# Four weight tiles instead of three in the slab-wise first products of a two-layer decoder trunk, and a later row broadcast

## The chip, the core and the metric

One core of a Trainium2 chip runs the whole program. Its engines have queues of their own: PE (TensorE: matmuls), DVE (VectorE), ACT (ScalarE), POOL (GpSimd) and SP, which issues most loads. The metric is the device time of one execution in microseconds. Before the change it is 2145.63 us, the median of three runs (2145.09 to 2147.61).

## What is computed

A decoder trunk of two layers over 512 positions of width 1024, in float32. Each layer has four sub-layers, and each of these adds a normalised output to the residual x:

```
for i in range(DEPTH):                                   # 2
    h = rmsnorm(x, g_ffn1_pre[i])
    x = x + 0.5 * rmsnorm(swiglu(h, w1_gate[i], w1_up[i], w1_down[i]), g_ffn1_post[i])   # 1024 -> 2816 -> 1024
    h = rmsnorm(x, g_mix_pre[i])
    ... = split(h @ w_in[i])                             # three head groups: two attentions, a short convolution
    x = x + rmsnorm(concatenate([y_sb, y_mla, y_cv]) @ w_out[i], g_mix_post[i])
    h = rmsnorm(x, g_ffn2_pre[i])
    x = x + 0.5 * rmsnorm(swiglu(h, w2_gate[i], w2_up[i], w2_down[i]), g_ffn2_post[i])
    h = rmsnorm(x, g_ple_pre[i])
    e = sigmoid(h @ w_ple_gate[i]) * (p[i] @ w_ple_proj[i])
    x = x + rmsnorm(e, g_ple_post[i])
```

with `rmsnorm(x, g) = x * rsqrt(mean(x * x) + 1e-6) * g`.

## The kernel before

Everything is held transposed: 128 channels on the partitions, the 512 positions along the free side, so x is eight tiles (slabs, k = 0 to 7) of 128 x 512. A float32 product is made of three matmuls of rounded halves: high weights with high activations, high weights with low activations, low weights with high activations (`product`, L286 to L288). High halves of weights (wh) are casts on ACT (L270), low halves (wl) a subtraction on DVE or POOL (L271); one such instruction covers 128 x 512, four slabs of a tile. A weight tile is 1024 x 128: eight slabs, two loads of 256 KB, two wh and two wl. There are 4 buffers for raw loads and 8 each for wh and wl, so four whole tiles at a time.

At the seven boundaries between sub-layers the work is split in two halves of the positions, A and B (256 columns each). The old stage ends in `finish`: its output is scaled by the reciprocal root of its mean square. For each half, the roots rt are worked out by nine small DVE instructions (L369), spread over the partitions by transposes on PE (L402, "the row"), copied by ACT (L403, rbs), and multiplied into the output (L579, DVE and POOL by turns). Then x is updated (L583 or L586), and the new stage's input is split: the high half xh on ACT (L467), the low half xl on DVE (L470), and ACT squares x for the next norm. `Entry` does this: `half` for one half, slab by slab.

The new stage doesn't wait for its own norm. `Entry.products` multiplies the first `FIRST` weight tiles with half A slab by slab, as soon as a slab is there: for each slab k the products of xh with wh and wl of every tile (L488, L489), and one slab later (`LAG`) those of xl with wh (L493). This order on PE is written out by hand. After slab `ROW_AT` comes the row of half B of the old stage (`row_b`), which DVE needs to start on half B; the rest of half A follows. Half B of the same tiles comes then, by `product`. `more` adds `MORE` further tiles, whole: 24 matmuls of 512 columns each; their casts and subtractions are held back by `later` until the last high and low half of half A are issued. Then the sums of squares of both halves go through PE as one-column matmuls (st, L389), DVE makes the new stage's own roots, and their row (the "full row") is broadcast when the stage calls `state.row()`.

The FFN computes eight tiles in plain products before its main loop: tiles 0 to 2 in `products`, 3 in `more`, 4 and 5 before the full row and 6 and 7 behind it. The mixer has four tiles before the value products (vt, L1111 to L1113): three in `products`, one in `more`. The embedding (`ple`) has three tiles and eight projections in `more`. The first FFN of layer 0 has no stage before it and uses a start of its own with three tiles. All other instructions are ordered by a scheduler that works from priorities and its own estimates; only the PE and DVE parts marked `manual_schedule` are fixed.

The letters in `ON_FFN1`, `ON_FFN2`, `ON_MIX` and `ON_PLE` say for each tile where its two wl are made: v on DVE, g on POOL.

Of the kernel before, what the change touches and what calls it, by code (L numbers as in the profile page):

```python
# [33 lines left out]
AT_END = (8, 16)  # L34

FIRST = 3
ROW_AT = 5
MORE = 1
LAG = 1
PROJ = 8  # L40
LAST_POOL = (2, 6)
DIRECT = 2

ON_FFN1 = 'vv gg vg'
ON_FFN2 = 'vv vv vv'
ON_MIX = 'vg vg vg'
ON_PLE = 'vv vg vg'
ON_IN = 'vv'
ON_VT = 'v'
# [52 lines left out]
PLAIN_BANKS = "zsfzzsdf"  # L102
# [56 lines left out]
def hybrid_trunk(ctx: ExitStack, tc: tile.TileContext, a: dict, out: bass.AP):  # L159
# [9 lines left out]
    def slot(dt=F32, name="s", tag="s"):  # L169
        return sp.tile([P, S], dt, tag=tag, name=name, bufs=SLOTS[tag])  # L170
# [6 lines left out]
    def bank(name="ps", tag=None):  # L177
        if tag is None:
            tag = dense[0][turn[0] % len(dense[0])]
            turn[0] += 1  # L180
        return ps.tile([P, S], F32, tag=tag, name=name, bufs=BANKS[tag])
# [13 lines left out]
    def split(src, tag="s"):  # L195

        h, lo = slot(F32R, "h", tag), slot(F32R, "l", tag)
        A.copy(out=h, in_=src)
        V.tensor_tensor(out=lo, in0=src, in1=f(h), op=ALU.subtract)  # L199
        return h, lo  # L200
# [26 lines left out]
    def round_constants():  # L227
        tri = slot(name="tri")
        nc.scalar.dma_start(out=tri, in_=a["const"][:, C_MS:C_MS + 4 * P])
        A.copy(out=conr[:, 0:P], in_=ident)  # L230
        A.copy(out=conr[:, P:5 * P], in_=tri)
# [12 lines left out]
    def load_w(src, slabs, cols, on="vv", tag=None):  # L244


        per = S // cols
        return [w for k0 in range(0, slabs, per)
                for w in halves(load_raw(src[:, k0:min(k0 + per, slabs)], cols), on[k0 // per % len(on)], tag)]
# [29 lines left out]
    def product(o, w, xs, first=True, cols=slice(0, S), tick=lambda: None, last=True):  # L279

        oc = o[:, cols]
        n = len(xs)
        for k in range(n):
            (wh, wl), (xh, xl) = w[k], xs[k]
            kw = dict(skip_group_check=True)
            T.matmul(oc, wh, xh[:, cols], start=first and k == 0, stop=False, **kw)  # L286
            T.matmul(oc, wh, xl[:, cols], start=False, stop=False, **kw)  # L287
            product.last = T.matmul(oc, wl, xh[:, cols], start=False, stop=last and k == n - 1, **kw)  # L288
            tick()

    def start():

        def load(t, c):
            m, j = divmod(t, 2)
            raw[t, c] = load_raw(a["w1_gu"][0, m, j][:, 4 * c:4 * c + 4], P)

        def part(k):
            g = gain(0, "ffn1_pre", k)
            h, lo = xs[k]
            A.activation(out=h, in_=x[k], func=AF.Copy, scale=g)  # L300
            V.scalar_tensor_tensor(out=lo, in0=x[k], scalar=g, in1=f(h), op0=ALU.mult, op1=ALU.subtract)

        xs = [(slot(F32R, "xh"), slot(F32R, "xl")) for _ in range(NK)]
        raw, w = {}, {}
        for k, tc_ in enumerate(((0, 0), (1, 0), (0, 1), (1, 1))):
            load(*tc_)
            load_x(k + 1)
        load_x(*range(5, NK))
        load_constants()
        for k, t in enumerate(((0, 0), (1, 0), (0, 1), (1, 1))):  # L310
            part(k)
            w[t] = halves(raw[t])
        for k, c in ((4, 0), (6, 1)):
            load(2, c)
            part(k)
            w[2, c] = halves(raw[2, c])
            part(k + 1)
        first = [(w[t, 0] + w[t, 1], bank("ps", PLAIN_BANKS[t])) for t in range(3)]
        for k in range(NK):
            for w_, o in first:  # L320
                product(o, w_[k:k + 1], xs[k:k + 1], k == 0, last=k == NK - 1)
        sq = Squares()
        for k in range(NK):
            sq.add(x[k])
        sq.fold()
        eps = eps_col()
        r = Rstd(D, keep=eps)
        r.add(*sq.parts(), last=True)
        r.col()
        behind = rsqrt_cols.last.ins  # L330

        def row():
            rb = slot(name="rb")
            r.row(rb, "v")
            return rb

        return SimpleNamespace(xs=xs, row=row, first=first, eps=eps, behind=behind)
# [112 lines left out]
    class Entry:  # L450
# [27 lines left out]
        def products(self, tiles, more=lambda: None):  # L478
# [3 lines left out]
            with tc.manual_schedule(engines={T.engine}):  # L482

                for k in range(NK + LAG):
# [5 lines left out]
                    if k >= LAG:  # L490
                        j = k - LAG
                        for w, o in tiles:
                            T.matmul(o[:, ca], w[j][0], self.xs[j][1][:, ca], start=False, stop=j == NK - 1, **kw)  # L493
                    if k == ROW_AT:
                        self.row_b()
# [236 lines left out]
    def ffn(l, idx, state, nxt, xtag="s", early=None):  # L732
# [4 lines left out]
        order = [(m, j) for m in range(PLAIN) for j in range(2)]  # L737
        src = a[f"w{idx + 1}_gu"]

        def weights(m, j, on="vv"):  # L740
            return load_w(src[l, m, j], NK, P, on)
# [17 lines left out]
            banks[m, j] = b  # L759

        def more():
            for i in range(FIRST, FIRST + MORE):
                with state.later():
                    w = weights(*order[i])
                banks[order[i]] = bank("ps", PLAIN_BANKS[i])
                product(banks[order[i]], w, xs)
# [5 lines left out]
            u.load("t1")  # L772
            u.load("t3")
        if l == 0 and idx == 0:
            first, done = state.first, FIRST
            round_constants()
        else:
            first = [(weights(*t, on), bank("ps", b))
                     for t, on, b in zip(order[:FIRST], (ON_FFN1, ON_FFN2)[idx].split(), PLAIN_BANKS)]
            state.products(first, more)  # L780
            done = FIRST + MORE
        for t, (_, b) in zip(order, first):
            banks[t] = b
        forms = input_forms(l, f"ffn{idx + 1}_pre", xs, xtag)
# [47 lines left out]
        for m in range(NK - LAST_DOWN):  # L832
            if early is not None and m == TRIG_AT:
                early()
            if m < TOGETHER:
                o = together[m]
            else:
                o = bank()
# [211 lines left out]
    def mixer(l, state, nxt):  # L1050
# [9 lines left out]
        def scaled(o, r, name="c"):  # L1060
            c = slot(name=name)
            V.tensor_tensor(out=c, in0=o, in1=r, op=ALU.mult)
            return c

        def latent(ms, name):
# [9 lines left out]
            if name[4] in FOLD:  # L1075
# [2 lines left out]

        q, kk = [], []
        first = [(load_w(a["win_f"][l, m], NK, P, on), bank("in", t))  # L1080
                 for m, t, on in zip((5, 6, 7, 8)[:FIRST], "zzzf", ON_MIX.split())]
        rest = []

        def more():
            for m, t in ((5, "z"), (6, "z"), (7, "z"), (8, "f"))[FIRST:]:
                with state.later():
                    w = load_w(a["win_f"][l, m], NK, P)
                rest.append(bank("in", t))
                product(rest[-1], w, xs)

        state.products(first, more)
        rt, rb = state.rt, state.row()
        for i in range(4):
            o = first[i][1] if i < FIRST else rest[i - FIRST]
            if i < 2:
                c = slot(name="c")
                V.scalar_tensor_tensor(out=c, in0=o, scalar=0.125, in1=rb, op0=ALU.mult, op1=ALU.mult)
                q.append(split(c, "m"))
            else:
                kk.append(split(scaled(o, rb), "m"))  # L1100
# [17 lines left out]
        for b in range(TB):  # L1118
            o = vt[b]
# [152 lines left out]
        for m in range(NK - LAST_OUT):  # L1272
            o = bank("wo")
# [69 lines left out]
    state = start()  # L1343
    for l in range(DEPTH):
        state = ffn(l, 0, state, (l, "mix_pre"), xtag="m" if l else "s", early=None if l else trig)
        state = mixer(l, state, (l, "ffn2_pre"))
        state = ffn(l, 1, state, (l, "ple_pre"))
        state = ple(l, state, (l + 1, "ffn1_pre") if l + 1 < DEPTH else None)
# [58 lines left out]
```

## Time and profile before

| | |
|---|---|
| median of 3 runs | 2145.63 us |
| the profiled execution | 2147.86 us |
| its span, first to last instruction | 2146.1 us |
| mean granted PE clock | 0.984 |
| PE busy | 2059.6 us, 96% |
| DVE busy | 1553.6 us, 72% |
| ACT busy | 1116.6 us, 52% |
| POOL busy | 506.6 us, 24% |

The profile is of one execution, whose time is 2.2 us over the median. Times in the trace count from the first instruction. A row of the timeline has its start, its duration, engine, line and operation, what is written and read, the shape, and in brackets the engine's idle time before it and what ended that. L numbers are lines of the kernel before; in the changed kernel every line after the constants is two further on.

### The profile page before, as it was taken

The numbers are of one execution on the slowest core, as the hardware profiler recorded it, in microseconds if no ns is written. First come the engines' busy times: TensorE is split into PE (matmuls) and PEld (weight loads), VectorE is DVE, ScalarE is ACT, GpSimd is POOL, SyncE is SP. The second block draws the span as 40 slices with busy tenths as digits, with TensorE's granted clock in tenths as the row PEclk, the third lists the DMA queues.
The fourth block names the chain that finished last, engine by engine and source line by source line (L and its number), as shares of the span: only waits on it lengthen the run. The fifth ranks groups of instructions, "written<-read, shape, count | busy, mean of one in ns | idle before, by whom it ended". The sixth has DMA issues, their size and how long they took to land.

```text
span 2146.1 us, 35942 instructions
## 1 busy us (share of the span) xinstructions
PE 2059.6 (96%) x13264; PEld 1874.2 (87%) x13264; DVE 1553.6 (72%) x2851; ACT 1116.6 (52%) x2296; POOL 506.6 (24%) x498
## 2 busy tenths in 40 slices
PE   8999999999989999999989999999999899999996
PEld 6999988887888999888879998888878889998886
DVE  7888754778878788636798786357788798885376
ACT  6556533555656555524565555235455565564243
POOL 3111012126432111003431110031263421100043
PEclk9999999999999999999999999999999999999998
DMA  7777332211133876332427763322111348753321
GB/s 218 172 180 177 89 104 72 91 60 52 55 79 108 196 173 148 100 99 79 122 84 196 178 163 93 98 68 93 53 59 46 88 126 192 180 137 96 98 73 65
DMA packets 139425, 244.73 MB, mean 114 GB/s; under 512 B 15600, under 2 KB 26096, under 8 KB 139248
## 3 DMA queue, kind: packets, MB, share of 16 engines
q1 hardware_dynamic: 117792, 204.00, 30.9%
q0 software_dynamic: 20736, 37.76, 11.2%
q8 instruction: 104, 1.70, 0.3%
q10 hardware_dynamic: 720, 0.67, 0.1%
q14 instruction: 73, 0.60, 0.1%
HBM read 240.27 MB, written 2.10 MB: 113 GB/s over the span
## 4 chain that ended last, share of the span: by engine, by line
PE 82%; DVE 12%; ACT 2%; issue 1%; DMA 1%; POOL 0%; SPq 0%; DVEq 0%; ACTq 0%; POOLq 0%
PE ps L286 9%; PE ps L287 9%; PE ps L288 9%; PE ux L698 6%; PE ux L697 6%; PE ux L696 6%; PE uy L698 3%; PE uy L697 3%; PE uy L696 3%; PE in L286 2%; PE in L287 2%; PE in L288 2%; DVE xl L470 2%; DVE wl L271 2%; PE uz L698 2%; PE uz L697 2%
## 5 line engine op out<-in xcount | busy, mean ns | idle before, releaser
L271 DVE TENSOR_TENSOR wl<-raw,wh 128x512 fp32r<-128x512 f32 (+2 forms) x893 | 605.8, 692 | 393.4 <-ACT wh L270 340.8
L270 ACT CAST wh<-raw 128x512 fp32r<-128x512 f32 (+1 forms) x934 | 548.7, 605 | 577.9 <-PE ps L287 275.1
L444 POOL TENSOR_TENSOR sq<-sq 128x256 f32<-128x256 f32 (+1 forms) x165 | 172.6, 1046 | 730.5 <-ACT sq L434 726.3
L287 PE MATMUL ps<-l,wh 128*128 128x512 f32 (+1 forms) x824 | 302.2, 367 | 0.0
L288 PE MATMUL ps<-h,wl 128*128 128x512 f32 (+1 forms) x824 | 301.8, 367 | 0.4 <-DVE wl L271 0.4
L286 PE MATMUL ps<-h,wh 128*128 128x512 f32 (+1 forms) x824 | 300.2, 368 | 0.0
L680 POOL DMA_DIRECT2D raw<-in_w_gu x144 | 125.9, 915 | 678.0 <-DMA raw<-in_w_gu 181.8
L698 PE MATMUL ux<-fh,wl 128*128 128x256 f32 x864 | 244.5, 283 | 0.0
L697 PE MATMUL ux<-fl,wh 128*128 128x256 f32 x864 | 244.5, 283 | 0.0
L696 PE MATMUL ux<-fh,wh 128*128 128x256 f32 x864 | 244.4, 283 | 0.0
L288 PEld LDWEIGHTS ps<-h,wl 128*128 128x128 f32 x824 | 155.4, 189 | 25.9 <-DVE wl L271 1.3
L287 PEld LDWEIGHTS ps<-l,wh 128*128 128x128 f32 x824 | 155.5, 189 | 24.8 <-DVE l L199 0.2
L286 PEld LDWEIGHTS ps<-h,wh 128*128 128x128 f32 x824 | 155.4, 189 | 24.6
L696 PEld LDWEIGHTS ux<-fh,wh 128*128 128x128 f32 x864 | 165.8, 192 | 0.5
L697 PEld LDWEIGHTS ux<-fl,wh 128*128 128x128 f32 x864 | 165.8, 192 | 0.5
L698 PEld LDWEIGHTS ux<-fh,wl 128*128 128x128 f32 x864 | 165.8, 192 | 0.0
L286 PE MATMUL ps<-xh,wh 128*128 128x512 f32 (+1 forms) x416 | 133.3, 356 | 15.5 <-ACT wh L270 9.8
L287 PE MATMUL ps<-xl,wh 128*128 128x512 f32 (+1 forms) x416 | 142.0, 352 | 1.2 <-DVE xl L470 1.2
L288 PE MATMUL ps<-xh,wl 128*128 128x512 f32 (+1 forms) x416 | 142.2, 350 | 0.0
L286 PEld LDWEIGHTS ps<-xh,wh 128*128 128x128 f32 x416 | 77.4, 196 | 28.7 <-ACT wh L270 11.2
L686 DVE TENSOR_TENSOR raw<-raw 128x512 f32<-128x512 f32 x144 | 98.6, 684 | 0.1
L287 PEld LDWEIGHTS ps<-xl,wh 128*128 128x128 f32 x416 | 80.6, 194 | 10.4 <-DVE xl L470 2.0
(347 smaller groups left out, 5237.1 us busy)
## 6 DMA issues: line engine op xcount, KB each, us to landing
raw<-in_w_gu SPq DMA_DIRECT2D x424, 256.0 KB, 4.0
raw<-in_w_down SPq DMA_DIRECT2D x160, 256.0 KB, 2.7
raw<-in_w_gu POOLq DMA_DIRECT2D x144, 256.0 KB, 5.1
raw<-in_win_f SPq DMA_DIRECT2D x60, 256.0 KB, 2.7
raw<-in_ple_gate SPq DMA_DIRECT2D x32, 256.0 KB, 2.7
raw<-in_wo_a SPq DMA_DIRECT2D x18, 256.0 KB, 2.8
raw<-in_w_down SPq DMA_DIRECT2D x32, 128.0 KB, 2.2
raw<-in_wo_b SPq DMA_DIRECT2D x12, 256.0 KB, 2.7
```

What stands on the lines that cost most here:

```text
L270: A.copy(out=h, in_=raw)
L271: (G if on == "g" else V).tensor_tensor(out=lo, in0=raw, in1=f(h), op=ALU.subtract)
L286: T.matmul(oc, wh, xh[:, cols], start=first and k == 0, stop=False, **kw)
L287: T.matmul(oc, wh, xl[:, cols], start=False, stop=False, **kw)
L288: product.last = T.matmul(oc, wl, xh[:, cols], start=False, stop=last and k == n - 1, **kw)
L444: G.tensor_tensor(out=self.acc[:, c], in0=self.acc[:, c], in1=self.last[:, c], op=ALU.add)
L470: iv = V.scalar_tensor_tensor(out=lo, in0=x[k][:, c], scalar=g, in1=f(h), op0=ALU.mult, op1=ALU.subtract)
L680: G.dma_start(out=self.raw[n], in_=self.part(m), accum_op=ALU.add)
L686: V.tensor_tensor(out=r, in0=r, in1=self.raw[p], op=ALU.add)
L696: T.matmul(o, wh, xh, start=first and k == 0, stop=False, **kw)
L697: T.matmul(o, wh, xl, start=False, stop=False, **kw)
L698: T.matmul(o, wl, xh, start=False, stop=k == 3, **kw)
```

## The change

`FIRST` stays 3 for the embeddings. FFN and mixer get constants of their own with 4, `MORE` becomes 0, so the fourth tile goes through the two halves like the others, and its casts and subtractions are no longer held back. `ROW_AT` goes from 5 to 7 at all seven boundaries. The fourth entry 'vv' puts both wl of the fourth tile on DVE, where `more` had them too.

```diff
@@ -34,16 +34,18 @@
 AT_END = (8, 16)
 
 FIRST = 3
-ROW_AT = 5
-MORE = 1
+FIRST_FFN = 4
+FIRST_MIX = 4
+ROW_AT = 7
+MORE = 0
 LAG = 1
 PROJ = 8
 LAST_POOL = (2, 6)
 DIRECT = 2
 
-ON_FFN1 = 'vv gg vg'
-ON_FFN2 = 'vv vv vv'
-ON_MIX = 'vg vg vg'
+ON_FFN1 = 'vv gg vg vv'
+ON_FFN2 = 'vv vv vv vv'
+ON_MIX = 'vg vg vg vv'
 ON_PLE = 'vv vg vg'
 ON_IN = 'vv'
 ON_VT = 'v'
@@ -759,7 +761,7 @@
             banks[m, j] = b
 
         def more():
-            for i in range(FIRST, FIRST + MORE):
+            for i in range(FIRST_FFN, FIRST_FFN + MORE):
                 with state.later():
                     w = weights(*order[i])
                 banks[order[i]] = bank("ps", PLAIN_BANKS[i])
@@ -772,13 +774,13 @@
             u.load("t1")
             u.load("t3")
         if l == 0 and idx == 0:
-            first, done = state.first, FIRST
+            first, done = state.first, len(state.first)
             round_constants()
         else:
             first = [(weights(*t, on), bank("ps", b))
-                     for t, on, b in zip(order[:FIRST], (ON_FFN1, ON_FFN2)[idx].split(), PLAIN_BANKS)]
+                     for t, on, b in zip(order[:FIRST_FFN], (ON_FFN1, ON_FFN2)[idx].split(), PLAIN_BANKS)]
             state.products(first, more)
-            done = FIRST + MORE
+            done = FIRST_FFN + MORE
         for t, (_, b) in zip(order, first):
             banks[t] = b
         forms = input_forms(l, f"ffn{idx + 1}_pre", xs, xtag)
@@ -1078,11 +1080,11 @@
 
         q, kk = [], []
         first = [(load_w(a["win_f"][l, m], NK, P, on), bank("in", t))
-                 for m, t, on in zip((5, 6, 7, 8)[:FIRST], "zzzf", ON_MIX.split())]
+                 for m, t, on in zip((5, 6, 7, 8)[:FIRST_MIX], "zzzf", ON_MIX.split())]
         rest = []
 
         def more():
-            for m, t in ((5, "z"), (6, "z"), (7, "z"), (8, "f"))[FIRST:]:
+            for m, t in ((5, "z"), (6, "z"), (7, "z"), (8, "f"))[FIRST_MIX:]:
                 with state.later():
                     w = load_w(a["win_f"][l, m], NK, P)
                 rest.append(bank("in", t))
@@ -1091,7 +1093,7 @@
         state.products(first, more)
         rt, rb = state.rt, state.row()
         for i in range(4):
-            o = first[i][1] if i < FIRST else rest[i - FIRST]
+            o = first[i][1] if i < FIRST_MIX else rest[i - FIRST_MIX]
             if i < 2:
                 c = slot(name="c")
                 V.scalar_tensor_tensor(out=c, in0=o, scalar=0.125, in1=rb, op0=ALU.mult, op1=ALU.mult)
```

The order of DVE at the boundary into mixer 0, before: y is the last output of the old FFN, x_75 to x_78 are slabs 2 to 5 of x.

```order
L470 SCALAR_TENSOR_TENSOR xl<-x_74,gains,xh 128x256
L855 TENSOR_SCALAR y<-ps,half 128x256
L586 TENSOR_TENSOR x_76<-y,x_76 128x256
L470 SCALAR_TENSOR_TENSOR xl<-x_75,gains,xh 128x256
L579 TENSOR_TENSOR y<-y,rbs 128x256
L586 TENSOR_TENSOR x_77<-y,x_77 128x256
L470 SCALAR_TENSOR_TENSOR xl<-x_76,gains,xh 128x256
L586 TENSOR_TENSOR x_78<-y,x_78 128x256
L369 SCALAR_TENSOR_TENSOR r_v<-st,eps 128x2
```

And in the changed kernel at the same place:

```order
L472 SCALAR_TENSOR_TENSOR xl<-x_74,gains,xh 128x256
L857 TENSOR_SCALAR y<-ps,half 128x256
L588 TENSOR_TENSOR x_76<-y,x_76 128x256
L273 TENSOR_TENSOR wl<-raw,wh 128x512 x2
L472 SCALAR_TENSOR_TENSOR xl<-x_75,gains,xh 128x256
L581 TENSOR_TENSOR y<-y,rbs 128x256
L371 SCALAR_TENSOR_TENSOR r_v<-st,eps 128x2
L588 TENSOR_TENSOR x_77<-y,x_77 128x256
L472 SCALAR_TENSOR_TENSOR xl<-x_76,gains,xh 128x256
```

Two wl, those of the fourth tile, now stand between the updates of slab 3 and the low half of slab 2; in the order before they stand behind half A:

```order
L369 TENSOR_TENSOR r_q<-r_v,r_z 128x2
L470 SCALAR_TENSOR_TENSOR xl<-x_80,gains,xh 128x256
L369 TENSOR_TENSOR r_q<-r_q,r_z 128x2
L369 SCALAR_TENSOR_TENSOR r_w<-r_q 128x2
L271 TENSOR_TENSOR wl<-raw,wh 128x512
L369 SCALAR_TENSOR_TENSOR rt<-r_w,r_z 128x2
L271 TENSOR_TENSOR wl<-raw,wh 128x512
L579 TENSOR_TENSOR y<-y,rbs 128x256
L586 TENSOR_TENSOR x_73<-y,x_73 128x256
```

These rows became:

```order
L371 TENSOR_TENSOR r_q<-r_v,r_z 128x2
L472 SCALAR_TENSOR_TENSOR xl<-x_79,gains,xh 128x256
L371 TENSOR_TENSOR r_q<-r_q,r_z 128x2
L371 SCALAR_TENSOR_TENSOR r_w<-r_q 128x2
L472 SCALAR_TENSOR_TENSOR xl<-x_80,gains,xh 128x256
L371 SCALAR_TENSOR_TENSOR rt<-r_w,r_z 128x2
L581 TENSOR_TENSOR y<-y,rbs 128x256
L588 TENSOR_TENSOR x_73<-y,x_73 128x256
L588 TENSOR_TENSOR x_74<-y,x_74 128x256
```

The two wl are gone from there, and the row's L581 follows rt at once.

PE at the same boundary (the output is the mixer's bank in). Before, a slab has three pairs of xh products, with no other matmul between them; the last two pairs of slab 1, the xl products and the start of slab 2:

```order
L488 MATMUL in<-xh,wh 128x256
L489 MATMUL in<-xh,wl 128x256
L488 MATMUL in<-xh,wh 128x256
L489 MATMUL in<-xh,wl 128x256
L493 MATMUL in<-xl,wh 128x256 x3
L488 MATMUL in<-xh,wh 128x256
```

In the changed kernel, the third and fourth pair of slab 0 and the first of slab 1 (st are one-column sums of squares for half B of the old stage):

```order
L490 MATMUL in<-xh,wh 128x256
L491 MATMUL in<-xh,wl 128x256
L490 MATMUL in<-xh,wh 128x256
L391 MATMUL st<-con,sq 128x1 x2
L491 MATMUL in<-xh,wl 128x256
L490 MATMUL in<-xh,wh 128x256
L491 MATMUL in<-xh,wl 128x256
```

The fourth tile's pair of products stands in slab 0, with two of the sums between its two matmuls. At the row of half B, before:

```order
L489 MATMUL in<-xh,wl 128x256
L493 MATMUL in<-xl,wh 128x256 x3
L402 MATMUL rb<-ident,rt 128x128 x2
L488 MATMUL in<-xh,wh 128x256
L489 MATMUL in<-xh,wl 128x256
```

and in the changed kernel:

```order
L491 MATMUL in<-xh,wl 128x256
L495 MATMUL in<-xl,wh 128x256 x4
L404 MATMUL rb<-ident,rt 128x128 x2
L495 MATMUL in<-xl,wh 128x256 x4
L288 MATMUL in<-xh,wh 128x256 x4
```

The row now has only the last slab's four xl products behind it before half B begins.

DVE at the boundary into the second FFN of layer 0 (part is the mixer's output), before:

```order
L579 TENSOR_TENSOR part<-part,rbs 128x256
L1287 TENSOR_TENSOR part<-wo,part 128x256
L583 SCALAR_TENSOR_TENSOR x_75<-part,gains,x_75 128x256
L470 SCALAR_TENSOR_TENSOR xl<-x_74,gains,xh 128x256
L583 SCALAR_TENSOR_TENSOR x_76<-part,gains,x_76 128x256
L470 SCALAR_TENSOR_TENSOR xl<-x_75,gains,xh 128x256
L579 TENSOR_TENSOR part<-part,rbs 128x256
L369 TENSOR_SCALAR r_v<-st 128x2
```

and in the changed kernel:

```order
L581 TENSOR_TENSOR part<-part,rbs 128x256
L1289 TENSOR_TENSOR part<-wo,part 128x256
L273 TENSOR_TENSOR wl<-raw,wh 128x512
L585 SCALAR_TENSOR_TENSOR x_75<-part,gains,x_75 128x256
L273 TENSOR_TENSOR wl<-raw,wh 128x512
L472 SCALAR_TENSOR_TENSOR xl<-x_74,gains,xh 128x256
L585 SCALAR_TENSOR_TENSOR x_76<-part,gains,x_76 128x256
L472 SCALAR_TENSOR_TENSOR xl<-x_75,gains,xh 128x256
L581 TENSOR_TENSOR part<-part,rbs 128x256
```

Here too the two wl of the fourth tile move into half A, one ahead of the update of slab 2 and one behind it.

## The prediction

> **What bounds the kernel now.** I read the page first, then the waits, then windows and the timeline around the seven stage boundaries. From the page and the waits (engine line waited for: us in total, times, longest us):
>
> ```profile
> span 2146.1 us, 35942 instructions
> PE 82%; DVE 12%; ACT 2%; issue 1%; DMA 1%; POOL 0%; SPq 0%; DVEq 0%; ACTq 0%; POOLq 0%
> PE rb L402 <- DVE rt L369: 27.2, 10, 4.4
> ```
>
> PE carries the chain, and DVE takes it over for 12%. The third line names one such place: PE waits for the reciprocal roots rt before it can broadcast them (L402). Seven of its ten cases are row b of the half-entries (start, us, engine and line, in brackets the idle time before and what ended it):
>
> ```profile
> 378.08 0.43 PE L402 MATMUL rb<-ident,rt 128*128 128x128 f32 x2 [3.91 <-DVE rt L369]
> 645.62 0.69 PE L402 MATMUL rb<-ident,rt 128*128 128x128 f32 x2 [3.56 <-DVE rt L369]
> 1010.87 0.43 PE L402 MATMUL rb<-ident,rt 128*128 128x128 f32 x2 [1.93 <-DVE rt L369]
> 1083.49 0.69 PE L402 MATMUL rb<-ident,rt 128*128 128x128 f32 x2 [4.44 <-DVE rt L369]
> 1444.58 0.69 PE L402 MATMUL rb<-ident,rt 128*128 128x128 f32 x2 [2.93 <-DVE rt L369]
> 1713.69 0.69 PE L402 MATMUL rb<-ident,rt 128*128 128x128 f32 x2 [3.56 <-DVE rt L369]
> 2076.18 0.43 PE L402 MATMUL rb<-ident,rt 128*128 128x128 f32 x2 [1.93 <-DVE rt L369]
> ```
>
> In this order: mixer 0, second FFN 0, embedding 0, first FFN 1, mixer 1, second FFN 1, embedding 1; 22.3 us of PE idle. Whether that is time of the kernel depends on who is bound on both sides. Windows (stretch: us, then busy time of PE, PEld, DVE, ACT, POOL, PE clock, DMA share, GB/s), mixer 0 and second FFN 0, each up to row b and behind it:
>
> ```profile
> 363.80:378.08 14.28, 8.27 (x65) 7.66 (x65) 14.14 (x31) 7.75 (x19) 8.49 (x10) 1.00 0.05 13
> 378.08:396.70 18.62, 18.62 (x122) 17.58 (x123) 16.38 (x28) 9.52 (x25) 9.30 (x11) 0.91 0.22 60
> 631.00:645.62 14.62, 9.93 (x76) 9.04 (x76) 14.59 (x33) 10.28 (x25) 10.42 (x12) 0.97 0.12 35
> 645.62:677.06 31.44, 31.44 (x176) 28.32 (x176) 30.65 (x57) 20.62 (x46) 11.68 (x13) 0.90 0.38 105
> ```
>
> Up to row b DVE is the bound (14.14 of 14.28, 14.59 of 14.62). Behind it the mixer is PE's (18.62 of 18.62), while in the FFN both are full (DVE 30.65 of 31.44). So a filled row wait is no gain as such: it gives PE work that it then need not do later, which helps only where PE is the later of the two.
>
> **The change part by part. PE's work** stays nearly equal:
>
> ```profile
> 365.55 0.28 PE L488 MATMUL in<-xh,wh 128*128 128x256 f32 x1
> 365.67 0.28 PE L489 MATMUL in<-xh,wl 128*128 128x256 f32 x1
> 379.01 0.42 PE L488 MATMUL in<-xh,wh 128*128 128x256 f32 x1
> 379.22 0.41 PE L489 MATMUL in<-xh,wl 128*128 128x256 f32 x1
> 395.10 0.39 PE L286 MATMUL in<-xh,wh 128*128 128x512 f32 x1
> 395.33 0.39 PE L287 MATMUL in<-xl,wh 128*128 128x512 f32 x1
> ```
>
> Matmuls follow each other every 0.12 us with 256 columns and every 0.23 with 512. The fourth tile's 24 x 0.23 = 5.5 us become 48 x 0.12 = 5.8: +0.3 per boundary. Rows three and four are the same matmul 0.21 apart: after a mostly idle stretch PE runs at half clock for a window.
>
> **The fourth tile's weights come late.** Its first low halves (wl, a DVE subtraction for four slabs) stand in DVE's new order where the front part shows them, in the middle of half A's updates. DVE in mixer 0 and second FFN 0:
>
> ```profile
> 368.19 0.47 DVE L855 TENSOR_SCALAR y<-ps,half 128x256 f32<-128x256 f32 x1
> 368.59 0.41 DVE L586 TENSOR_TENSOR x<-y,x 128x256 f32<-128x256 f32 x1
> 368.92 0.96 DVE L470 SCALAR_TENSOR_TENSOR xl<-x,gains,xh 128x256 fp32r<-128x256 f32 x1
> 377.26 0.69 DVE L271 TENSOR_TENSOR wl<-raw,wh 128x512 fp32r<-128x512 f32 x1
> 635.35 0.41 DVE L1287 TENSOR_TENSOR part<-wo,part 128x256 f32<-128x256 f32 x1
> 635.69 0.64 DVE L583 SCALAR_TENSOR_TENSOR x<-part,gains,x 128x256 f32<-128x256 f32 x1
> ```
>
> Mixer 0: the two wl go in where L470 started, 368.92; the first is done 0.65 later, at 369.55. PE's order is written by hand: slab 0 now has an eighth matmul that needs this wl, at the place where 365.67 stands. PE waits there some 3.9 us; the idle time moves from row b to slab 0. From 369.55 on, one matmul of slab 0, 7 x 8 of slabs 1 to 7 and 7 x 4 low products come before row b: 85 x 0.12 = 10.2, so row b stands at 379.75 at the earliest, 1.7 later than now; rt (two wl of 0.65 ahead of it, one that stood before it gone) moves by 0.65 to about 378.6 and is no longer what PE waits for. If the stall sets the clock to half up to 371.8, as after the row waits now, it is 1.1 more. DVE's half B starts 1.7 to 2.8 later. Second FFN 0: wl at 635.69 + 0.65 = 636.35, plus 10.2, plus 1.45 for the twelve one-column sums that stand there: row b at 648.0, or 649.4 with half clock, against 645.62. DVE's start of half B:
>
> ```profile
> 378.95 0.42 DVE L579 TENSOR_TENSOR y<-y,rbs 128x256 f32<-128x256 f32 x1 [0.33 <-ACT rbs L403]
> 645.49 1.28 DVE L271 TENSOR_TENSOR wl<-raw,wh 128x512 fp32r<-128x512 f32 x2
> 646.75 0.42 DVE L579 TENSOR_TENSOR part<-part,rbs 128x256 f32<-128x256 f32 x1
> ```
>
> In the FFN the row takes about 0.9 us to reach DVE, and now two wl fill those; they have moved forward, so DVE really waits there. Its start goes from 646.75 to 648.9 (full clock) or 650.3: **+2.1 to +3.5**. What it meets later:
>
> ```profile
> 675.77 0.16 DVE L369 SCALAR_TENSOR_TENSOR rt<-r_w,r_z 128x4 f32<-128x4 f32 x1
> 676.20 0.69 DVE L271 TENSOR_TENSOR wl<-raw,wh 128x512 fp32r<-128x512 f32 x1 [0.27 <-issue]
> 682.60 1.29 DVE L271 TENSOR_TENSOR wl<-raw,wh 128x512 fp32r<-128x512 f32 x2 [1.05 <-ACT wh L270]
> 685.24 0.47 PE L286 MATMUL ps<-xh,wh 128*128 128x512 f32 x1 [2.12 <-DVE g L751]
> ```
>
> DVE is busy nearly without a gap from 646.75 to the full row's rt, the wl at 676.20 frees the buffer whose next load feeds 682.60, and PE waits 2.12 us for what follows. This chain passes DVE's shift on. I take +2.8 in layer 0. In layer 1 the sums stand elsewhere and the row moves from 1713.69 to about 1716.1, with DVE +2.1 behind it: I take +2.1, between 0 and +3.5 (half clock). The 0 would come if PE decided: behind row b it has 21 + 72 + 48 matmuls of 0.12 now (the fourth tile's 24 counted twice) and 4 + 96 then, 4.9 us less.
>
> **The mixer absorbs it**, being PE-bound behind the row:
>
> ```profile
> 391.51 0.47 DVE L470 SCALAR_TENSOR_TENSOR xl<-x,gains,xh 128x256 fp32r<-128x256 f32 x1
> 393.71 0.40 PE L286 MATMUL in<-xh,wh 128*128 128x512 f32 x1
> 396.46 0.95 PE L389 MATMUL st<-con,sq 128*128 128x1 f32 x8
> 397.27 0.38 PE L1111 MATMUL vt<-wh,xh 128*128 128x288 f32 x1
> 397.62 0.29 PE L1113 MATMUL vt<-wh,xl 128*128 128x288 f32 x1
> 397.75 0.29 PE L1111 MATMUL vt<-wh,xh 128*128 128x288 f32 x1
> ```
>
> Now the last low half is done at 391.98, half B of three tiles ends at 393.7, then twelve matmuls of the fourth, eight sums, and the values start at 397.27. Changed: last low half at 394.7, half B of four tiles 1.7 x 4/3 = 2.3 later, 397.0, the sums 0.8: 397.8; but nine of the value matmuls (0.13 each, 1.2 us) stand ahead of that in PE's new order. That is 396.6 against 397.27: -0.6, between -2.5 (no slab-0 stall) and +1.5 (the value matmuls wait too). The same for mixer 1.
>
> **First FFN 1** gets its fourth weights in time: the stage before keeps three tiles and leaves buffers free, and two wl go from ahead of rt, so row b comes near 1083.2. Against it, POOL's new order puts a wl ahead of the sum that PE awaits here:
>
> ```profile
> 1058.88 0.61 PE L389 MATMUL st<-con,sq 128*128 128x1 f32 x4 [2.16 <-POOL sq L444]
> ```
>
> -0.6 for the row, +0.6 for the sum: 0, between -1 and +1.2. **The embeddings** change only in ROW_AT: two slabs of 9 matmuls, 18 x 0.12 = 2.2 us, fill the wait of 1.93, and row b is 0.2 later. I take 0, between -1.9 (all the wait comes back) and +0.5, each. The attention's POOL, ACT and DVE orders also differ in places; PE is the bound there and I take 0, within 2 either way. SP issues the same loads in the same order.
>
> Sum: 2.8 + 2.1 - 0.6 - 0.6 + 0 + 0 = **+3.7 us**. The profiled execution took 2147.86 us (span 2146.1), so it would take 2151.6; it lies 2.2 over the median of the three runs, 2145.63, and on that scale the forecast is **2149.3 us**, +0.17%. A measurement of this kernel tells 0.2% (4.3 us) from no change, so this is no change, near the edge to slower.
>
> The Trainium skill, "TensorE: Matmul & The Clock Gate", Part 1, What's actually happening, says that the clock drops to half after an idle window of about 3.4 us on a free-running grid. The trace halves it sooner: the two transposes at 1444.58 last 0.69 us where those at 378.08 last 0.43, behind a wait of only 2.93 us. By the page's rule a stall of 3 to 3.9 us, astride two windows, would mostly cost no clock: the FFN terms would be +2.1 and +2.1, the mixers -1.7 each, and the sum +0.8.
>
> **Rivals.** (1) Faster: the stall at slab 0 is small, since the scheduler's order is not the time at which a wl runs; with the weights there, row waits and the half clock after them go. The mixers gain 2.5 each, first FFN 1 1.0, the embeddings 1.9 each, the second FFNs 1 to 2 each: about -12, 2134. For it: 22.3 us of waits and PE's full windows. Against: DVE runs in order and is full up to the row. Chance 0.24, with times from 2130 to 2141.
>
> (2) Slower: everything is passed on. If in the mixers the last low half of half B comes over 0.6 us later than worked out, the value matmuls stand behind it and PE's slack is gone: +1.5 each; with half clock in both second FFNs +3.5 each, first FFN +1.2, embeddings +0.5 each: +12, 2158. Chance 0.15.
>
> (3) Nothing: DVE makes up the shift, since the fourth tile needs no two wl there any more and PE is 5 us ahead: the FFN terms vanish, and -1.2 is left, 2144.4. Or the clock stays full behind the stalls: row b is 1.1 earlier in the mixers and 1.4 in the second FFN 0, +0.8 in all, 2146.4 (the case in which the page's rule would hold). Chances 0.10 and 0.08.
>
> **The numbers.** The forecast's own range (2145 to 2152) has 0.43, of which 0.23 within 0.2% and 0.20 above it; with (3) and its two cases 0.41 are within 0.2%, with (2) 0.35 slower, and with (1) 0.24 faster. The range from 2136 to 2156 leaves out the far ends of both rivals.
>
> **What would show it.** Right: in mixer 0 and second FFN 0 a PE wait of 3 to 4 us inside slab 0, ended by DVE's wl, and none before row b; DVE's first L579 of half B 2 to 3 us later against the slab's start; the tile-7 wait still there. Wrong: no stall at slab 0 (rival 1 then), or a row wait that stays, or a full row in the second FFNs that comes no later.

## The result and the profile after

The changed kernel takes 2171.85 us, the median of four runs (2169.64 to 2178.95), against 2146.62 us for the kernel before: a ratio of 1.0125, with a 95% interval of 1.0109 to 1.0141. The forecast was no change, 2149.3 us, in a range that ended at 2156. It was wrong in size, and it had put at nothing the places where most of the loss lies.

From the page of the changed kernel and its list of waits (engine and line waited for: us in total, times, longest; lines are two higher than before):

```profile
span 2167.9 us, 36175 instructions
PE 83%; DVE 11%; ACT 2%; issue 2%; DMA 1%; POOL 0%; SPq 0%; DVEq 0%; ACTq 0%; POOLq 0%
PE rb L404 <- DVE rt L371: 12.0, 7, 3.7
PE st L391 <- ACT sq L535: 10.3, 6, 3.2
PE ps L491 <- DVE wl L273: 5.7, 2, 2.9
PE ps L288 <- ACT xh L469: 5.5, 3, 1.8
PE vm L1186 <- DVE kf L1234: 3.2, 2, 1.6
```

The waits for rt have fallen from 27.2 to 12.0 us, as they should. New ones stand in their place: the fourth tile's wl in slab 0 (L491) and the sums beside it (L391), the wait behind the row (L288 for xh), and one in the attention (vm for kf), which the edit doesn't touch.

To see where the 21.8 us of the two spans lie, the program is cut at points that both traces share, by PE's timeline:

| stretch (us) | before | after | difference | forecast |
|---|---|---|---|---|
| start to the first FFN's main loop | 61.23 | 58.78 | -2.45 | 0 |
| mixer 0, entry to the last value product | 45.79 | 47.68 | +1.9 | -0.6 |
| attention and output product 0 | 221.62 | 226.56 | +4.9 | 0 |
| second FFN 0, entry to its main loop | 60.16 | 62.23 | +2.1 | +2.8 |
| embedding 0 and first FFN 1, with the loops around | 435.35 | 435.94 | +0.6 | 0 |
| mixer 1, entry to the last value product | 46.69 | 46.79 | +0.1 | -0.6 |
| attention and output product 1 | 222.10 | 226.88 | +4.8 | 0 |
| second FFN 1, entry to its main loop | 57.43 | 63.49 | +6.1 | +2.1 |
| its main loop to the end, with embedding 1 | 388.36 | 392.20 | +3.8 | 0 |

The main loop and down product of each first FFN agree within 0.02 us. The first row is the same code in both kernels; it lay between 58.1 and 61.2 us in all kernels run here, with a window of half clock in the profile of before. It is no effect of the change.

The forecast stall is there. PE in second FFN 0 of the changed kernel (start, us, engine, line, operation; in brackets the idle time before):

```profile
640.78 0.39 PE L491 MATMUL ps<-xh,wl 128*128 128x256 f32 x1 [2.87 <-DVE wl L273]
...
642.86 2.55 PE L391 MATMUL st<-con,sq 128*128 128x1 f32 x12
645.27 0.56 PE L490 MATMUL ps<-xh,wh 128*128 128x256 f32 x1
...
655.49 0.38 PE L404 MATMUL rb<-ident,rt 128*128 128x128 f32 x2
...
658.19 0.74 PE L288 MATMUL ps<-xh,wh 128*128 128x256 f32 x4 [1.83 <-ACT xh L469]
```

PE waits 2.87 us in slab 0 for DVE's wl, then runs at half clock (from 641.9 to 648.7): the twelve sums take 2.41 us to the next product. Row b follows without a wait, 655.49 - 636.74 = 18.75 us after the first slab's start; before it was 645.62 - 632.37 = 13.25. (The windows further down count from the last output product, 0.12 us earlier.) And behind the row PE has only four products left, then 1.83 us of nothing: the row has to pass ACT, DVE and ACT again before half B has its first slab. Before, two slabs stood there and filled that time.

### The profile page after: what moved, and what is told of

It is laid out like the page before. It is cut to its first block, busy times and chain, and to the rows that moved or that the text cites. A ratio compares the mean times of both kernels' runs of the same rounds, so it can differ in the third digit from the quotient of the medians.

```text
span 2167.9 us, 36175 instructions
## 1 busy us (share of the span) xinstructions
PE 2073.9 (96%) x13384; PEld 1886.7 (87%) x13384; DVE 1564.5 (72%) x2851; ACT 1113.4 (51%) x2296; POOL 512.1 (24%) x498
## 4 chain that ended last, share of the span: by engine, by line
PE 83%; DVE 11%; ACT 2%; issue 2%; DMA 1%; POOL 0%; SPq 0%; DVEq 0%; ACTq 0%; POOLq 0%
PE ps L288 10%; PE ps L289 10%; PE ps L290 10%; PE ux L700 6%; PE ux L699 6%; PE ux L698 6%; PE uy L699 3%; PE uy L700 3%; PE uy L698 3%; PE in L289 2%; PE in L288 2%; PE in L290 2%; DVE wl L273 2%; PE uz L699 2%; PE uz L698 2%
## 5 line engine op out<-in xcount | busy, mean ns | idle before, releaser
L288 PE MATMUL ps<-h,wh 128*128 128x512 f32 (+1 forms) x824 | 300.9, 369 | 1.0 <-ACT wh L272 1.0
L288 PEld LDWEIGHTS ps<-h,wh 128*128 128x128 f32 x824 | 155.6, 189 | 26.3 <-ACT wh L272 1.8
L288 PE MATMUL ps<-xh,wh 128*128 128x512 f32 (+1 forms) x416 | 132.2, 353 | 19.3 <-ACT wh L272 9.6
L289 PE MATMUL ps<-xl,wh 128*128 128x256 f32 (+1 forms) x416 | 141.3, 350 | 1.9 <-DVE xl L472 1.9
L288 PEld LDWEIGHTS ps<-xh,wh 128*128 128x128 f32 x416 | 76.7, 199 | 30.9 <-ACT wh L272 10.8
```

## The experiments

All were timed against the kernel before on the same chip. Stretches are read from the traces as in the table above.

### Four tiles, the row after slab 5 again

```diff
-ROW_AT = 7
+ROW_AT = 5
```

> The changed kernel with ROW_AT back at 5, four tiles kept. Theory 1 (the loss has three sources: the stall at slab 0 with the half clock behind it in the second FFNs; an attention order that the scheduler changes only where four tiles and a later row meet in the mixer, 4.5 and 4.8 us; the later row in the embeddings, about 4 us): the attention from the values to the output product takes as long as before, within 1 us, the last embedding too, and some +2 to +8 us are left from the second FFNs: 2148 to 2155 us. Theory 2 (the fourth tile as such costs it all, the row's place nothing): 2165 us or more.

2140.96 us against 2144.89, ratio 0.998 (0.9968 to 0.9992). With the row after slab 5 the fourth tile costs nothing: there is no loss without the later row. Theory 1 was right that the attentions don't stay long (220.2 and 221.7 us), but missed in the total, since the second FFNs, for which it left 2 to 8 us, took 58.1 and 58.7 us against 60.2 and 57.4. PE in second FFN 0 of this kernel:

```profile
632.27 0.38 PE L491 MATMUL ps<-xh,wl 128*128 128x256 f32 x1 [2.85 <-DVE wl L273]
...
643.30 0.43 PE L404 MATMUL rb<-ident,rt 128*128 128x128 f32 x2 [2.14 <-DVE rt L371]
```

The stall in slab 0 is the same, 2.85 us. Yet PE comes to the row too early and waits 2.14 us more for rt. The stall takes time that PE has.

A second measurement, in more rounds:

> The kernel with four tiles and the row after slab 5 everywhere, once more, in more rounds. If four tiles gain by themselves: 0.997 to 0.999 of the kernel before, as measured first. If the first measurement was the clock's luck (mixers or FFNs alone gave 0.9998): 0.9995 to 1.0005.

2144.77 us against 2145.76, ratio 0.9993 (0.9983 to 1.0002): between the two cases, and not told from no change. The two intervals overlap at 0.9983 to 0.9992. The two profiles of this one kernel also show what the clock does to a single stage: second FFN 0 took 58.1 us in the first, with 3.4 us at half clock, and 60.2 in the second, with 13.7.

### The row after slab 5 in the mixers alone, or the embeddings alone

```diff
-                    if k == ROW_AT:
+                    if k == ROW_AT[self.name[:3]]:
```

with `ROW_AT = {"ffn": 7, "mix": 5, "ple": 7}`, then with `{"ffn": 7, "mix": 7, "ple": 5}`.

> The changed kernel with the row after slab 5 in the mixers alone. Theory 1: the attention's order is that of before again, and both attentions lose their 4.5 and 4.8 us against the changed kernel: 2160 to 2164 us, with the second FFNs and the last embedding as in the changed kernel. Theory 2 (the attention is late for another reason, such as the clock or the fourth tile's buffers): 2169 to 2173 us.

2149.26 us, ratio 1.002 (1.001 to 1.003): 22.6 us less than the changed kernel, more than twice what was expected. The attentions with their output products take 221.3 and 221.7 us, the mixers' entries 45.4 and 45.5, the second FFNs 58.6 and 61.8. By the spans the changed kernel is 19.7 us longer than this one: 10.4 in the two attentions, 3.5 in the mixers' entries, and 5.3 in the second FFNs, whose instructions on PE stand in the same order in both.

> The changed kernel with the row after slab 5 in the embeddings alone. Theory 1: the end of the program, from the first product of the last embedding on, takes 3 to 4 us less than in the changed kernel, as before: 2166 to 2169 us. Theory 2 (the end differs because of what came earlier, such as the position of the clock's windows): the end keeps its length, 2170 to 2173 us.

2166.64 us, ratio 1.01 (1.0085 to 1.0115), as theory 1 had it. From the last embedding's first product to the end it was 3.4 us shorter, and the stretch with embedding 0 1.4. What it costs there is seen in embedding 1. Before, on DVE and PE, and then in the changed kernel:

```profile
2098.88 0.16 DVE L369 SCALAR_TENSOR_TENSOR rt<-r_w,r_z 128x4 f32<-128x4 f32 x1
2100.76 0.60 PE L402 MATMUL rb<-ident,rt 128*128 128x128 f32 x4
```

```profile
2119.58 0.16 DVE L371 SCALAR_TENSOR_TENSOR rt<-r_w,r_z 128x4 f32<-128x4 f32 x1
2123.04 0.60 PE L404 MATMUL rb<-ident,rt 128*128 128x128 f32 x4
2125.04 0.50 PE L288 MATMUL ps<-xh,wh 128*128 128x512 f32 x1 [1.40 <-DVE g L1315]
```

Counted from the embedding's first xh product (2061.35 and 2079.29), the full row moves from 39.4 to 43.75 us: rt is 2.8 us later, and then lies 3.3 us in place of 1.7 behind PE's other products. The gates start that much later, and PE waits 1.40 us for the first.

### The later row with three tiles

```diff
-FIRST_FFN = 4
-FIRST_MIX = 4
+FIRST_FFN = 3
+FIRST_MIX = 3
 ROW_AT = 7
-MORE = 0
+MORE = 1
```

> The kernel before with ROW_AT 7 at all boundaries and three tiles as before: the later row alone. Theory 1 (the later row costs through the attention's changed order, which needs four tiles as well, and in the embeddings): the attentions as before within 1 us, the embeddings +1 and +3 to +4, the other boundaries within 1.5 us: 2148 to 2152 us. Rival (the later row costs the same with three tiles): 2157 us or more, with the attentions 4 us longer.

2149.6 us, ratio 1.0024 (1.0013 to 1.0036). The time is as expected, but the attentions were 3.1 and 2.6 us longer with their output products, not the same. This is a miss of theory 1. Each of the two stretches held 10.2 us at half clock, and the profiled execution took 2155.98 us, 6.4 more than the median; the comparison of orders below puts the miss down to the clock.

### The row after slab 7 in one kind of stage alone, with four tiles

```diff
-ROW_AT = {"ffn": 7, "mix": 5, "ple": 7}
+ROW_AT = {"ffn": 5, "mix": 7, "ple": 5}
```

> Four tiles, the row after slab 7 in the mixers alone and after slab 5 in FFNs and embeddings. Theory 1: against four tiles with row 5 everywhere (2141.0 us) the two attentions are 4 to 7 us longer each, the mixers' entries 2 to 4 each: 2153 to 2161 us. Rival (the loss needs the later row in several boundaries together): 2141 to 2147 us.

2164.27 us, ratio 1.0089 (1.0074 to 1.0104), slower than expected. The mixers alone bring 23.3 us over four tiles with the row after slab 5 (19.5 over their second measurement). Attention and output product take 230.8 and 226.7 us, the mixers' entries 47.9 and 46.8.

The same with `{"ffn": 7, "mix": 5, "ple": 5}`:

> Four tiles, the row after slab 7 in the FFNs alone and after slab 5 in mixers and embeddings. Theory 1 (in the FFNs the later row costs little by itself: 1 to 4 us in all, from the wait behind the row and the clock): attention and last embedding as before, 2142 to 2146 us. Rival (the FFN's row b, 5 to 7 us later in the changed kernel, passes on in full at each of three boundaries): 2151 us or more.

2144.31 us, ratio 1.0 (0.9989 to 1.0011). Three FFNs in which the row goes after slab 7 cost nothing that can be told from no change. Windows over second FFN 0 and 1 of this kernel, and of the changed kernel (stretch: us, busy of PE, PEld, DVE, ACT, POOL, PE clock, DMA share, GB/s):

```profile
631.43:690.33 58.90, 50.73 (x317) 45.50 (x316) 55.14 (x105) 38.70 (x84) 22.81 (x24) 0.97 0.29 87
1692.84:1752.11 59.27, 52.14 (x317) 46.76 (x316) 55.35 (x105) 38.76 (x84) 22.78 (x24) 0.94 0.28 86
```

```profile
636.74:698.85 62.11, 54.94 (x316) 49.53 (x315) 55.27 (x105) 38.41 (x84) 22.02 (x23) 0.89 0.28 82
1712.31:1775.68 63.37, 55.44 (x316) 49.90 (x315) 54.85 (x105) 38.52 (x84) 22.59 (x23) 0.89 0.27 79
```

PE's instructions stand in the same order in both, and DVE's busy time agrees within 0.5 us. In layer 0 the stretch takes 58.9 us in one and 62.1 in the other, at a granted clock of 0.97 and 0.89. Two more kernels have this order, mix_row5 and ple_row5. Over the eight stages the time goes with the time at half clock: 58.6 and 58.9 us with 3.4 us of it, 59.3 and 61.2 with 6.8, 61.6 and 61.8 with 10.2, 62.2 and 63.5 with 13.7, the last two of them the changed kernel's.

### The fourth tile three slabs later

```diff
-                for k in range(NK + LAG):
+                for k in range(NK + LAG + DELAY * (len(tiles) > 3)):
...
+                    for n, (w, o) in enumerate(tiles):
+                        i = k - DELAY * (n == 3)
+                        if 0 <= i < NK:
```

with `DELAY = 3`; the xl products of that tile move with it.

> The changed kernel with the fourth tile's slab products placed three slabs later in PE's order of half A (its slab 0 beside slab 3 of the others), so that its weights are there when PE comes to them; everything else as in the changed kernel. Theory 1: no wait for the low half in slab 0, row b of the second FFNs 3 to 6 us earlier against the slab's start, and 5 to 8 us less in all, since the attention's order stays the changed one: 2163 to 2167 us. Rival (DVE's half A and its chain decide, the stall only shows it): row b and the time stay within 2 us, 2169 to 2173 us.

2165.76 us, ratio 1.0092 (1.0075 to 1.0108), 6.1 us less than the changed kernel. The wait for wl is gone; the time is inside what theory 1 expected, and the attentions stay long (228.2 and 229.3). Row b of the second FFNs comes 2.4 and 4.7 us earlier than in the changed kernel, where 3 to 6 was expected.

> Four tiles, the row after slab 5 everywhere, and the fourth tile's slab products three slabs later in PE's order, so that its late weights stop nothing. Theory A (the prediction's: the stall at slab 0 costs): 2135 to 2138 us, 3 to 6 less than with the stall. Theory B (the stall takes idle time that PE has until rt in any case; with the row after slab 5 PE still waits 2 us for rt): within 1.5 us of the kernel with the stall, 2139.5 to 2142.5 us, and a longer wait at the row of half B.

2146.0 us, ratio 1.0005 (0.999 to 1.002): nothing gained by taking the stall away where the row stands after slab 5. Theory A falls. Theory B is right that it isn't worth anything, though not in its detail. The time is over its 2139.5 to 2142.5, which rested on the first measurement of the kernel with the stall; the second, 2144.77, is 1.2 us away. And in second FFN 0 PE's wait at row b is 0.72 us, not longer than 2.14, because PE now runs into the xh waits of the later slabs.

### Four tiles in one kind of stage, the row after slab 5

Both with `ROW_AT = 5`; first the mixers:

```diff
-FIRST_FFN = 4
+FIRST_FFN = 3
-MORE = 0
+MORE = 1
```

> Four tiles in the mixers alone, FFNs as before with three and one whole, the row after slab 5 everywhere. The fourth tile's gain in the mixers by the stages of the kernel with four tiles everywhere (entries 1.3 and 2.2 us shorter): 2141 to 2144.5 us. If the fourth tile alone gains nothing in the mixers (the stall at slab 0 takes what the row wait gives): 2144.5 to 2147 us.

2145.72 us, ratio 0.9998 (0.9987 to 1.001). Then the FFNs:

```diff
-FIRST_MIX = 4
+FIRST_MIX = 3
```

> Four tiles in the FFNs alone, mixers as before, the row after slab 5 everywhere. By the stages of the kernel with four tiles everywhere the second FFN of layer 0 is 2.0 us shorter, that of layer 1 1.3 longer, the first of layer 1 some 1 shorter: 2142 to 2145.5 us. By the prediction's terms for the second FFNs (+2.8 and +2.1) it would be 2148 us or more.

2146.41 us, ratio 0.9998 (0.9988 to 1.0009). Neither alone can be told from no change. For the mixers that is the second case, for the FFNs it lies between: their second entries took 61.0 and 58.3 us, +0.8 and +0.8 against before, not the forecast +2.8 and +2.1.

### What the mixers' row does to the attention

The order of PE in the attention is the same as before, but for one row in some, in all kernels whose mixers have the row after slab 5, and with three tiles also after slab 7. With four tiles and the row after slab 6 or 7 the scheduler puts it in another order: of PE's 538 rows between the last value product and the first output product of a layer, 99 stand elsewhere. Three kernels take order and lateness apart. The first has the row one slab earlier and the changed order (`ROW_AT = {"ffn": 5, "mix": 6, "ple": 5}`):

> Four tiles, the row after slab 6 in the mixers and after slab 5 elsewhere. The attention's instructions stand in the same order as with the row after slab 7. Theory order (the changed order of the attention costs most of the mixers' part): attention and output product together 4 to 10 us longer per layer than before, as with slab 7, 2153 to 2163 us. Rival (the lateness of the row itself costs, some 2 to 3 us per slab and mixer): about half of the 23 us between slab 5 and slab 7, 2147 to 2153 us.

2160.93 us, ratio 1.0071 (1.0054 to 1.0087). One slab of two gives back 3 of some 20 us: this speaks against lateness as what costs most.

The second has the row after slab 7 and, in the mixers, no lag of the xl products. In it, layer 0's attention is in the old order and layer 1's in the changed one:

```diff
-                for k in range(NK + LAG):
+                lag = LAG * (self.name[:3] != "mix")
+                for k in range(NK + lag):
```

> Four tiles, the row after slab 7 in the mixers and after slab 5 elsewhere, and in the mixers the low products in the same slab in place of one later. With that the attention of layer 0 stands in the order of the kernel before, that of layer 1 in the changed one. Theory order: layer 0's attention takes 112 to 114 us as before, layer 1's 116 to 120, and the total is 2150 to 2159 us. Rival (a late row makes the attention long in whatever order): both are 4 us or more longer, 2161 us or more.

2160.36 us, ratio 1.0056 (1.0036 to 1.0076). The total lies between the two cases and decides nothing, since both entries became 2.8 to 3.3 us longer than before. Layer 0's attention to the first output product took 115.6 us, not 112 to 114; layer 1's took 118.6, as expected.

The third has four tiles in the FFNs, three in the mixers, the row after slab 7 in the mixers, and the old order in both layers:

```diff
-FIRST_MIX = 4
+FIRST_MIX = 3
 ROW_AT = {"ffn": 5, "mix": 7, "ple": 5}
```

> Four tiles in the FFNs and three in the mixers, the row after slab 7 in the mixers and after slab 5 elsewhere. Here the attention of both layers stands in the order of before, with the late row. Theory order plus lateness (the late row costs some 3 us per attention and 1 to 2 per entry in whatever order, the changed order and the fourth tile the rest of the 23 us): 2151 to 2157 us, attention and output product together 2 to 4 us longer than before per layer. Rival (lateness alone): 2160 us or more. Rival (order alone): 2145 to 2149 us.

2147.9 us, ratio 1.0011 (1.0001 to 1.0021). The theory it was built for, order plus lateness, expected 2151 to 2157 and missed; order alone, 2145 to 2149, holds it. Against the same kernel with the mixers' row after slab 5 (2146.41, ratio 0.9998) a late row by itself, with three tiles in the mixers, costs about 1.5 us by the times and 2.8 by the ratios, not 20.

Windows over attention and output product of both layers, in this order: the changed kernel (both in the changed order), mix3_row7 (both in the old), mix_row7_lag0 (old, then changed):

```profile
410.06:636.62 226.56, 216.46 (x1173) 181.70 (x1172) 181.47 (x354) 121.01 (x265) 83.96 (x71) 0.99 0.24 70
1485.31:1712.19 226.88, 216.61 (x1174) 181.74 (x1172) 182.60 (x354) 120.63 (x265) 84.26 (x71) 0.99 0.24 70
```

```profile
408.68:629.88 221.20, 214.52 (x1174) 181.87 (x1173) 174.32 (x352) 120.87 (x264) 85.61 (x71) 0.99 0.24 71
1473.73:1695.12 221.39, 214.69 (x1173) 181.93 (x1172) 174.50 (x352) 120.87 (x264) 85.73 (x71) 0.99 0.24 71
```

```profile
411.81:636.50 224.69, 217.75 (x1173) 184.56 (x1172) 175.66 (x352) 120.76 (x264) 84.05 (x71) 0.98 0.24 70
1483.90:1712.10 228.20, 216.69 (x1173) 181.57 (x1172) 182.53 (x354) 120.97 (x265) 84.32 (x71) 0.99 0.24 69
```

The first number behind the stretch less PE's busy time is PE's idle time: 10.1 and 10.3 us in the changed order, 6.7 in the old, and in the third kernel 6.9 in the old and 11.5 in the changed. The old order's 224.69 has little idle time but a lower clock: three windows of half clock (10.2 us) lie in it, one in each of mix3_row7's stretches. Over all profiled kernels the stretch took 220.2 to 224.7 us in the old order (three over 222.1, each with 10.2 us at half clock) and 226.6 to 230.8 in the changed, with no overlap. Where each has one window of half clock (3.4 us) it is 220.7 to 222.1 against 226.6 to 228.3: **about 6 us per layer** for the order. That it is the order and not the fourth tile in the mixers rests on mix_row7_lag0, the one kernel with four tiles, a late row and the old order in one layer: there PE's idle time is that of the old order.

One place where part of it arises, on PE and DVE of layer 0, first in mix3_row7 and then in the changed kernel:

```profile
506.52 1.40 DVE L1234 TENSOR_TENSOR kf<-ko,rb 64x512 f32<-64x512 f32 x2
509.15 2.09 DVE L273 TENSOR_TENSOR wl<-raw,wh 128x384 fp32r<-128x384 f32 x1
514.42 0.50 PE L959 MATMUL z<-sph,conr 128*128 128x512 f32 x1 [1.99 <-DVE sph L189]
```

```profile
512.16 1.64 DVE L273 TENSOR_TENSOR wl<-raw,wh 128x384 fp32r<-128x384 f32 x1
513.72 1.40 DVE L1234 TENSOR_TENSOR kf<-ko,rb 64x512 f32<-64x512 f32 x2
512.29 0.50 PE L959 MATMUL z<-spl,conr 128*128 128x512 f32 x1 [1.13 <-DVE spl L192]
515.26 0.50 PE L1186 MATMUL vm<-wh,ch 128*128 128x512 f32 x1 [1.60 <-DVE kf L1234]
```

In the old order DVE takes kf ahead of the weight subtraction, and PE waits once. In the changed one kf stands behind it, and PE waits twice. The same two waits (1.13 or 1.14, 1.61) stand in mix_row6 and in layer 1 of mix_row7_lag0. This place alone makes 0.7 us: 1.13 + 1.60 against 1.99. Further waits of the changed order are 0.86 us for qf and 0.50 for the copy of a row, and the next wait for kf is 1.50 in place of 0.83. All of PE's idle time is 3.4 us more; the other 2 us of layer 0's 5.4 are longer busy time of PE, which no wait explains. A kernel with the changed order and an early row was not found, so this pairing of order and cost was not tried from that side.

## Why the prediction was wrong

**The bound and the row wait.** Right: up to row b DVE is the bound, and a filled row wait is no gain. The waits for rt fell by 15 us and nothing came of it.

**The fourth tile's weights come late.** The stall was forecast at 3 to 3.9 us in slab 0 and measured 2.87 in the second FFNs; in the mixers the one-column sums in the same slab stopped PE first, 2.93 us. But the step from there to the price failed. It charged the later DVE start to the stall. The same stall with the row after slab 5 costs nothing (2.85 us in four_row5, ratios 0.998 and 0.9993), and taking it away there gains nothing (delay3_row5). With the row after slab 7 at all boundaries, taking it away gains 6.1 us (delay3), in the mixers' entries and the second FFNs; there the time at half clock fell too, from 13.7 to 6.8 us in each second FFN. With stall and late row in the FFNs alone nothing was lost (ffn_row7), so how much of the 6.1 us is the stall and how much the clock stays open.

**The second FFNs.** +2.8 was +2.1 and +2.1 was +6.1. Up to the full row the mechanism was the forecast chain: counted from the last output product, row b came 5.5 and 7.0 us later than before, DVE's half B 5.2 and 6.6, the full row's rt 5.4 and 6.4. The size was the clock's. Where the same order ran at full clock up to the row (layer 0 of ffn_row7), row b came 15.79 us after that point, where the working has 648.0 - 632.25 = 15.75; in the changed kernel it came after 18.87 and 20.36. The working had allowed 1.4 us for half clock up to row b in layer 0. Against 15.79 it cost 3.1 and 4.6: two windows lay there in layer 0, and three in layer 1, from 1717.1 to 1727.3, in which products of half A and the sums lay. That layer 0 came out near its forecast is luck: its full row was 4.4 us later, and 2.3 us came back behind it, where the tile-7 wait of 2.12 us was gone. In layer 1 1.44 us of that wait stayed. With the later row in the FFNs alone the same stages cost nothing that could be measured (ffn_row7).

**"The attention's POOL, ACT and DVE orders also differ in places; PE is the bound there and I take 0, within 2 either way."** This is the step that failed most. It shows no row for that bound, and it doesn't name PE's own order, which changed as well. PE was busy 213.2 of 221.6 us there before, and the new order added waits all the same: two attentions cost 9.7 us in the profile, and about 6 each by the comparison at equal clock. With the entries and what follows them, the mixers' later row makes 22.6 of the 25 us (mix_row5). What part of that is the order and what the entries and the clock behind them isn't settled to better than a few us.

**The mixers absorb it.** Forecast -0.6 each, measured +1.9 and +0.1: inside the stated ends for mixer 1, just outside for mixer 0. In both PE idled 1.83 us behind the row, which the working had left out. The two differ by the clock: time at half clock went from 3.4 to 6.8 us in mixer 0, and from 10.2 to 3.4 in mixer 1.

**The embeddings.** Forecast 0, at most +0.5 each; measured 5.2 us for both together by the times (ple_row5), 4.8 by the stretches. The working looked at row b, which hardly moved, and not at the full row, which stands behind more of PE's products and came 4.3 us later in embedding 1.

**The clock.** The Trainium skill's idle window of about 3.4 us ("TensorE: Matmul & The Clock Gate", Part 1, What's actually happening) was weighed as a rival case. The runs don't bear it out as a lower bound: behind 2.87 us of idle time in slab 0 the sums took 2.41 us where the forecast had 1.45.

**The rivals.** The slower one named passed-on waits, with the mixers at +1.5 and the embeddings at +0.5 each; none of its parts was the attention.

## What to carry to other kernels

Filling a wait with work from behind it is free only if nothing needs that place behind: a broadcast has a latency of its own (2.7 us here, from row b to half B's first product in second FFN 0), and the work that used to cover it is gone when it is moved ahead. Where a scheduler orders the rest of the program, a row of differences far from the edit is a change of its own; price it as one, wait by wait, and test it by a variant that keeps the old order. A stall that comes before another wait on the same engine may cost nothing: ask what is late at the end of the stretch, not in it.

## What the runs showed of the hardware

The same PE instructions in the same order took 58.9 us in one kernel and 62.1 in another, at a granted clock of 0.97 and 0.89. The same kernel, profiled twice (four_row5 and four_row5_again), took 58.1 and 60.2 us there, with 3.4 and 13.7 us at half clock. So the difference isn't the edit's. What decides how many windows of half clock fall into a stretch was not tried. A window is 3.4 us long in these traces, and the time at half clock within the span came to 52 to 85 us per profile, so a single profile of a stretch with many short waits can be several us off.

In the changed order of the attention DVE was busy 181.5 and 182.6 us with the instructions that took 174.3 and 174.5 in mix3_row7, 2 records apart. The longer ones lie beside busy POOL. The same product of two tiles in layer 0, first in mix3_row7 and then in the changed kernel:

```profile
511.77 1.19 DVE L192 TENSOR_TENSOR u<-u,c 128x512 f32<-128x512 f32 x1
516.47 3.40 DVE L192 TENSOR_TENSOR u<-u,c 128x512 f32<-128x512 f32 x1
```

Its twin earlier in the layer, with POOL idle, takes 0.68 us in both kernels. In the changed kernel POOL's instructions follow each other without a gap from 511.65 to 521.0 us. Counted against the median of their shape, DVE's long instructions lose 16.9 us in each layer of mix3_row7 and 24.0 and 25.2 in the changed kernel, nearly all of it while POOL is busy for at least half of their time. What this costs PE was not tried.
